# A two-layer hybrid block on one core: the modulation's products pinned in VectorE's order, spread at new paces, and cut where a condition is unused

## The chip, the cores and the metric

The kernel runs on one core of one Trainium2 chip. The metric is the device time of one execution in microseconds, the median of several executions. The engines are called by the profile's names: PE (TensorE), PEld (its weight loads), DVE (VectorE), ACT (ScalarE), POOL (GpSimd) and SP (SyncE, which issues the DMAs). A line is called by its number in the kernel before: L495 is line 495.

## The reference, cut to what matters

Two layers work on 512 latent tokens (`x`) and 256 context tokens (`xc`) of 1024 features. Each layer first makes six modulation vectors for each of two conditions, `c` for the latent tokens and `c_ctx` for the context tokens, then runs four mixers side by side and a convolutional ffn:

```python
for i in range(DEPTH):                      # DEPTH = 2
    need_ctx = i < DEPTH - 1
    mod_l = split(silu(c) @ mod_w[i] + mod_b[i], 6)
    mod_c = split(silu(c_ctx) @ mod_w[i] + mod_b[i], 6)
    h_l = modulate(x, norm_mix_g[i], mod_l[0], mod_l[1])       # shift, scale
    h_c = modulate(xc, norm_mix_g[i], mod_c[0], mod_c[1])
    ...                                     # the mixers on h_l @ w_in[i], h_c @ w_in[i]
    x = x + mod_l[2] * (o_l @ w_out[i])                        # gate
    if need_ctx:
        xc = xc + mod_c[2] * (o_c @ w_out[i])
    x = x + mod_l[5] * conv_ffn(modulate(x, norm_ffn_g[i], mod_l[3], mod_l[4]), ...)
    if need_ctx:
        xc = xc + mod_c[5] * conv_ffn(modulate(xc, norm_ffn_g[i], mod_c[3], mod_c[4]), ...)
return x
```

In the last layer (`need_ctx` false) the context tokens are still normed and projected, as keys, values and states for the latent ones, but they have no output, gate or ffn.

## The kernel before, in words

**Layout.** Activations lie as [feature, token], 128 features on the partitions: 8 blocks of 1024 features, 768 tokens. On-chip memory is 30 slabs of 1536 columns that an allocator (`Arena`) hands out and takes back while the program is traced. Each product of matrices is made of three matmuls over a rounded part and a rest of each factor (`mm_feat`, L387). A weight comes in over SP's queue into one of three staging buffers (`weights`, L371), ACT rounds it (L377), POOL subtracts for the rest (L378), and both parts go into a ring of four slabs.

**Streams and clocks.** The order of the program is made by `weave`: generators run by turns, and the one whose clock is behind goes next. A generator advances its own clock by what it yields, a cost in nanoseconds written out by hand. Within the first layer's `weave` of the mixers there are five streams: the delta rule, gated linear attention (gla), the attentions, the projections, and `mod_part(0, 16, 48, 3500)`. The projections' clock goes on by 7776 for each of 11 feature blocks and by 6 x 2640 for each of 7 token blocks (L703). In the next `weave` the stream `last` does the output product, the norm, the ffn and the next layer's norm, and beside it `next_mod` waits for the flag "normed" and runs `mod_part(1, 0, 48, 8000)`. Within the ffn's clock each of 22 up steps yields twice 7800 and each of 8 parts of a down step over four blocks 4000; the last down step goes over six blocks. What is traced is then put into each engine's queue by a scheduler that works with its own forecast of times: an instruction that it holds to be ready may be queued ahead of others that were traced earlier. Each engine takes its queue in order, SP too.

**The modulation.** The 48 blocks of 128 modulation features of a layer are, eight at a time: shift, scale and gate of the mixers, then shift, scale and gate of the ffn. The first 16 blocks of the first layer are made at the very start (`mod_first`). All others are made on DVE by `mod_part`: a block's weights come as two loads of 128 x 512 on SP's queue (L493) into four buffers taken by turns, and for each of them and each of two conditions one SCALAR_TENSOR_TENSOR (L495) multiplies by the condition's silu and sums along the row into an accumulator. These are called products below. In the profile each product has two records, the operation and the read of its accumulator. When all blocks are done, two wide operations (L500, L501) add the halves and the bias. `silu_c` loads the two condition rows, makes their silu and keeps them in `self.sc` (two tiles of 1024 columns); `mod_part` frees them at its end, and `next_mod` makes them again.

**The ffn** (L593 to L678). An up step makes a block `u`, copies it (L610), makes a block `g`, convolves it over neighbouring tokens (ACT L617; DVE L620, L622), takes its silu (ACT L626; DVE L627, L628), and splits the result (ACT L631, POOL L632). After five up steps a down step multiplies the first four by their part of `w_down` and adds the product times the gate to `x` (DVE L651). The gate is half of the modulation vector 5, made by two operations (L603) at the ffn's start.

**The norm** takes its scale from the modulation by one operation (`scales`, L534); PE sums its squares (L547).

Of the kernel before, what the change touches and what calls it, by code (L numbers as in the profile page):

```python
# [16 lines left out]
ALU = mybir.AluOpType  # L17
# [3 lines left out]
L = 2  # L21
# [12 lines left out]
# per-partition parameter columns of one layer  # L34
# [8 lines left out]
# rows that are spread over the partitions  # L43
# [8 lines left out]
# blocks of w_in's columns: ("f", columns) gives [feature, token], ("t", columns) gives [token, feature]  # L52
# [21 lines left out]
# the first 16 blocks of the first layer's mod_w, and the engine of each  # L74
# [3 lines left out]
def _ptile(a):  # L78
    """[..., K*128] -> [..., 128, K]"""
    a = np.asarray(a)  # L80
    return np.moveaxis(a.reshape(a.shape[:-1] + (-1, P)), -1, -2)


def _kmajor(w):
    """[L, K*128, N] -> [L, 128, K, N]"""
    w = np.asarray(w)
    return w.reshape(w.shape[0], -1, P, w.shape[2]).transpose(0, 2, 1, 3)
# [75 lines left out]
class Arena:  # L163
    """column ranges of equal slabs, the longest unused first; a slab without tenants may change its kind"""
# [13 lines left out]
    def find(self, n, kind, low):  # L178
        """(slab, start) of n granules whose last use is the oldest, with a price on broken slabs"""
# [39 lines left out]
class Net:  # L219
# [3 lines left out]
    # per layer: the streams' paces (delta rule, its directions, gated linear attention, attentions, projections, modulation);  # L223
    # slabs that have to be unused before a step (front, direction, attention's part, its queries)
# [23 lines left out]
    # memory --------------------------------------------------------------  # L248
# [22 lines left out]
    def bank(self, n, lo, hi):  # L271
        """waits for n banks in a row out of lo .. hi - 1"""
# [27 lines left out]
    def weave(self, *streams, pace=(1.0,) * 8):  # L300
        """emits generators by turns: the one whose clock is behind goes first"""
# [12 lines left out]
    # constants and parameters -------------------------------------------  # L314
# [25 lines left out]
    # weights -------------------------------------------------------------  # L340
    def rings(self, slabs, stages):
        """buffers that weights take by turns"""
# [9 lines left out]
    def piece(self, n):  # L352
        """the next n columns of the ring, out of one slab"""
# [8 lines left out]
    def weights(self, src, nk, n):  # L362
        """nk blocks [128, n] of a weight: lists of their rounded and rest parts"""
# [17 lines left out]
    def mm_feat(self, ps, w, x, segs, cols=slice(None)):  # L381
        """ps[:, segments] = sum over k of w[k][:, cols]^T x[k], each product of two parts of two"""
# [7 lines left out]
    def mm_part(self, ps, w, x, spans, segs):  # L390
        """mm_feat, by spans that may become ready one after the other"""
        for a, b, _ in spans:
            self.mm_feat(ps, w, x, [(a, b)])
        if not spans:
            self.mm_feat(ps, w, x, segs)

    # rsqrt of a small tile by the bit estimate and Newton steps ----------
# [11 lines left out]
    def rstd(self, ms, mean, nm, eps=EPS):  # L409
        """(ms * mean + eps) ** -0.5 of a small tile"""  # L410
# [18 lines left out]
    # modulation ----------------------------------------------------------  # L429
# [6 lines left out]
    def silu_c(self):  # L436
        """silu of both conditions' rows, on all partitions"""
# [8 lines left out]
    def mod_first(self):  # L446
        """the first layer's shift and scale of the mixers, eight features' blocks by turns, over three engines"""
# [35 lines left out]
    def mod_part(self, li, m0, m1, dt):  # L483
        """blocks m0 .. m1 - 1 of 128 columns each: shift, scale, gate of the mixers, then of the ffn, eight blocks each"""
# [4 lines left out]
        part = self.new([m1 - m0, 2, 2])  # L489
        for m in range(m0, m1):  # L490
            for e in range(2):
                w = ws[(2 * m + e) % len(ws)]
                nc.sync.dma_start(out=w, in_=self.A["modw"][li * 48 + m - 16][:, e * hd:(e + 1) * hd])  # L493
                for s in range(2):
                    nc.vector.scalar_tensor_tensor(out=junk, in0=w, scalar=1.0, in1=self.sc[s][:, e * hd:(e + 1) * hd],  # L495
                                                   op0=ALU.mult, op1=ALU.mult, accum_out=part[:, m - m0, e, s:s + 1])
                yield dt / 2
        self.free(*ws, junk, *self.sc)
        mb = self.par(li, "modb", m0, m1 - m0)
        nc.vector.tensor_tensor(out=md[:, m0:m1], in0=part[:, :, 0], in1=mb.unsqueeze(2).to_broadcast([P, m1 - m0, 2]), op=ALU.add)  # L500
        nc.vector.tensor_tensor(out=md[:, m0:m1], in0=part[:, :, 1], in1=md[:, m0:m1], op=ALU.add)  # L501
        self.free(part)
        yield 100
# [5 lines left out]
    # norm and modulation: h = rms(x) * g * (1 + scale) + shift, split -----  # L509
    @staticmethod  # L510
    def spans(full):
        """ranges of tokens with their condition, two that may run one after the other"""
        return [(0, NL, 0), (NL, T, 1)] if full else [(0, NL // 2, 0), (NL // 2, NL, 0)]

    def squares(self, x, k, a, b, st):
        """adds the squares of x[k][:, a:b] to st["acc"], but for the last one's"""
# [10 lines left out]
    def norm(self, li, which, x, sts, h, parts, first=None):  # L527
        """the parts' spans one part after the other, each with its squares"""
        nc = self.nc
        sh, sc = (0, 1) if which == "nmg" else (3, 4)  # L530
        gs = self.small([P, 8, 2], "gs")

        def scales(k, m):
            nc.vector.scalar_tensor_tensor(out=gs[:, k:k + m], in0=self.mod[li][:, sc * 8 + k:sc * 8 + k + m], scalar=1.0,  # L534
                                           in1=self.par(li, which, k, m).unsqueeze(2).to_broadcast([P, m, 2]),
# [56 lines left out]
    # conv ffn --------------------------------------------------------------  # L592
    def ffn(self, li, x, h, done):  # L593
# [8 lines left out]
        for s in range(2):  # L602
# [1256 lines left out]
```

## Time and profile before

| | us |
|---|---|
| runs of the kernel before, median of 3 | 2450.39 |
| lowest and highest of them | 2445.48 and 2453.73 |
| span of the profiled execution, first to last instruction | 2445.8 |
| PE busy in it | 2211.0 (90%) |
| DVE busy | 1490.5 (61%) |
| POOL busy | 1047.3 (43%) |
| ACT busy | 937.5 (38%) |

Of the profiled execution only the span is given, no time of its own beside it. The span is 4.6 us below the median of the runs and inside their spread. Busy shares are means over stages that differ; the rows further down give them by stage. `PEclk` or "granted clock" is the share of TensorE's full clock that the chip granted; the clock has two levels, 1.2 and 2.4 GHz, so a mean between 0.5 and 1 is a mixture.

### The profile page before, as it was taken

What the parts mean: (1) busy time and instruction counts of PE and PEld (TensorE: products, weight loads), DVE (VectorE), ACT (ScalarE), POOL (GpSimd) and SP (SyncE); (2) the same over time, 40 slices, a digit from 0 to 9 for tenths busy, and PEclk for the clock granted to TensorE, in tenths of its full rate; (3) what the DMA queues carried; (4) which work ended last, traced back from release to release, by engine and by line L of the source; (5) the groups of instructions that cost most, each with busy time, mean ns of one, the idle gap of its engine ahead of it and who ended that gap; (6) DMA issues with size and microseconds to landing.
All of it is one profiled execution on the core that took longest, in us unless ns stands there. A gap on an engine that the chain in (4) does not pass through costs nothing. (4 is left out here: it accounts for less than half of the span.)

```text
span 2445.8 us, 40328 instructions
## 1 busy us (share of the span) xinstructions
PE 2211.0 (90%) x15292; PEld 1881.8 (77%) x15292; DVE 1490.5 (61%) x3201; ACT 937.5 (38%) x1758; POOL 1047.3 (43%) x1001
## 2 busy tenths in 40 slices
PE   4879898789979998969999999997989889999999
PEld 4767687677857787858888888786878778888888
DVE  6997568678764499994222262367778874423223
ACT  3322222256546342212232344323256564533333
POOL 3442356334221253334343464346433413555556
PEclk9889888799979999989999999898889999999999
DMA  7443134433224334542211142125533232222324
GB/s 250 168 151 119 47 126 121 109 95 84 74 73 139 101 113 148 172 153 70 67 63 61 61 157 70 48 67 148 135 90 83 59 122 95 87 94 95 98 93 138
DMA packets 232434, 259.54 MB, mean 106 GB/s; under 512 B 90992, under 2 KB 174256, under 8 KB 232240
## 3 DMA queue, kind: packets, MB, share of 16 engines
q1 hardware_dynamic: 232240, 256.97, 33.8%
q8 instruction: 120, 1.97, 0.3%
q14 instruction: 74, 0.61, 0.1%
HBM read 210.74 MB, written 37.77 MB: 102 GB/s over the span
## 5 line engine op out<-in xcount | busy, mean ns | idle before, releaser
L387 PE MATMUL pst<-slab,slab 128*128 128x512 f32 (+1 forms) x6552 | 1255.3, 353 | 55.0 <-ACT slab L631 20.8
L387 PEld LDWEIGHTS pst<-slab,slab 128*128 128x128 f32 x6552 | 1065.0, 193 | 239.3 <-ACT slab L631 21.4
L378 POOL TENSOR_TENSOR slab<-slab,slab 128x512 fp32r<-128x512 f32 (+1 forms) x428 | 584.0, 1374 | 728.5 <-ACT slab L377 685.0
L377 ACT CAST slab<-slab 128x512 fp32r<-128x512 f32 (+1 forms) x428 | 257.8, 612 | 538.0 <-PE pst L387 397.5
L703 PE MATMUL pst<-slab,slab 128*128 128x256 f32 (+1 forms) x1872 | 261.8, 302 | 17.9 <-POOL slab L378 17.7
L703 PEld LDWEIGHTS pst<-slab,slab 128*128 128x128 f32 x1872 | 250.4, 205 | 27.8 <-POOL slab L378 19.5
L620 DVE SCALAR_TENSOR_TENSOR slab<-pst,pp,slab 128x511 f32<-128x511 f32 x66 | 41.5, 657 | 312.6 <-ACT slab L617 312.6
L495 DVE SCALAR_TENSOR_TENSOR slab<-slab,slab 128x512 bf16<-128x512 f32 x240 | 227.6, 948 | 6.9 <-DMA slab<-in_modw_dram 0.8
L427 PE MATMUL pst<-cst,slab 128*128 128x128 f32 (+1 forms) x968 | 166.5, 305 | 60.0 <-POOL slab L1148 16.6
L427 PEld LDWEIGHTS pst<-cst,slab 128*128 128x128 f32 (+1 forms) x968 | 121.0, 153 | 88.0 <-DVE slab L859 20.0
L1545 PE MATMUL pst<-slab,slab 128*128 128x128 f32 (+5 forms) x1376 | 162.1, 278 | 9.1 <-DVE slab L1599 4.8
L651 DVE SCALAR_TENSOR_TENSOR slab<-pst,fgate,slab 128x512 f32<-128x512 f32 (+1 forms) x144 | 88.0, 629 | 127.5 <-PE pst L387 127.4
L1545 PEld LDWEIGHTS pst<-slab,slab 128*128 128x128 f32 (+3 forms) x1376 | 135.1, 176 | 29.8 <-issue 14.4
L940 DVE TENSOR_REDUCE mx<-pst 128x1 f32<-128x768 f32 (+1 forms) x120 | 100.2, 846 | 43.3 <-PE pst L937 20.6
L942 ACT ACTIVATE slab<-pst,mx 128x768 f32<-128x768 f32 (+1 forms) x120 | 97.9, 817 | 50.9 <-DVE mx L940 50.1
L632 POOL TENSOR_TENSOR slab<-slab,slab 128x768 fp32r<-128x768 f32 (+1 forms) x44 | 71.2, 1618 | 97.9 <-ACT slab L631 94.4
L626 ACT ACTIVATE slab<-slab 128x768 f32<-128x768 f32 (+1 forms) x44 | 32.4, 737 | 144.2 <-DVE slab L622 144.2
L495 DVE SCALAR_TENSOR_TENSOR slab<-slab 128x512 bf16<-128x512 f32 x80 | 73.5, 918 | 2.3
L1577 POOL TENSOR_TENSOR slab<-slab,pc 128x256 f32<-128x256 f32 x48 | 34.3, 727 | 87.6 <-PE pst L1545 16.0
L953 ACT ACTIVATE slab<-slab,r 128x768 f32<-128x768 f32 (+1 forms) x80 | 67.7, 853 | 8.7 <-DVE r L952 8.1
L970 PE MATMUL pst<-slab,slab 128*64 128x128 f32 x816 | 64.7, 291 | 3.8 <-ACT slab L422 1.7
L631 ACT CAST slab<-slab 128x768 fp32r<-128x768 f32 (+1 forms) x44 | 32.0, 728 | 92.1 <-DVE slab L628 92.0
(309 smaller groups left out, 2689.7 us busy)
## 6 DMA issues: line engine op xcount, KB each, us to landing
slab<-in_wup_dram SPq DMA_DIRECT2D x88, 512.0 KB, 3.4
slab<-in_modw_dram SPq DMA_DIRECT2D x160, 256.0 KB, 2.6
slab<-in_wdn_dram SPq DMA_DIRECT2D x48, 512.0 KB, 3.4
slab<-in_win_dram SPq DMA_DIRECT2D x46, 512.0 KB, 3.6
slab<-in_modw_dram SPq DMA_DIRECT2D x16, 512.0 KB, 7.0
slab<-in_wout_dram SPq DMA_DIRECT2D x16, 512.0 KB, 3.5
slab<-in_xT_dram SPq DMA_DIRECT2D x16, 384.0 KB, 5.7
kb<-slab SPq DMA_DIRECT2D x8, 768.0 KB, 4.2
```

The lines of the kernel that those rows point to most:

```text
L377: nc.scalar.copy(out=w[0], in_=st[:, k:k + q])
L378: nc.gpsimd.tensor_tensor(out=w[1], in0=st[:, k:k + q], in1=w[0].bitcast(F32), op=ALU.subtract)
L387: self.nc.tensor.matmul(ps[:, a:b], w[i][k][:, cols], x[j][k][:, a:b], start=(k == 0 and q == 0), stop=(k == nk - 1 and q == 2))
L427: self.nc.tensor.transpose(out, a.bitcast(F32) if a.dtype != F32 else a, self.c["ident"])
L495: nc.vector.scalar_tensor_tensor(out=junk, in0=w, scalar=1.0, in1=self.sc[s][:, e * hd:(e + 1) * hd], op0=ALU.mult, op1=ALU.mult, accum_ou ...
L632: nc.gpsimd.tensor_tensor(out=HL[:, 1, :n], in0=th[:, :n], in1=HL[:, 0, :n].bitcast(F32), op=ALU.subtract)
L651: nc.vector.scalar_tensor_tensor(out=x[m][:, a:b], in0=ps[:, a:b], scalar=gate[:, m, s:s + 1], in1=x[m][:, a:b], op0=ALU.mult, op1=ALU.add)
L703: self.nc.tensor.matmul(ps[:, :n], h[i][k][:, t * P:(t + 1) * P], w[j][k], start=(k == 0 and q == 0), stop=(k == KD - 1 and q == 2))
L940: nc.vector.tensor_reduce(out=mx, in_=sv, axis=AX.XY, op=ALU.max, negate=True)
L942: nc.scalar.activation(out=p[m][:, a:].rearrange("p (e c) -> p e c", e=2 - a // hb), in_=sv, func=AF.Exp, bias=mx, accum_out=lsum[:, m:m + 1])
L953: nc.scalar.activation(out=p[0][:, a:], in_=p[0][:, a:], func=AF.Copy, scale=r[:, 0:1])
L1545: mm = lambda o, a, b, pos: nc.tensor.matmul(o, a, b, start=True, stop=True, tile_position=pos)
```

## The change

`mod_part` takes a list of blocks instead of a range, adds the halves and the bias block by block, and no longer frees the condition rows. Each product is passed through the framework's `keep_in_program_order`, which adds an edge from the instruction that was traced last on the same engine: the product may not be queued on DVE ahead of it. The edge orders the queue and adds no semaphore wait. `conds` says how many conditions a block is made for: two, but one for the gates and the ffn's vectors of the last layer.

The blocks move. Beside the first layer's mixers run only blocks 16 to 39, at 8000 per block instead of 3500. Blocks 40 to 47, the first layer's ffn gate, run beside its ffn at 6000 per block, and behind them the 48 blocks of layer 2 at 9500 instead of 8000. The gate's two operations move from the ffn's start to the end of its fourth up step, behind a wait in the tracing for the flag "ffn gate". The silu of the conditions is made once.

```diff
-    def mod_part(self, li, m0, m1, dt):
+    def mod_part(self, li, ms, dt):
...
-        part = self.new([m1 - m0, 2, 2])
-        for m in range(m0, m1):
+        part = self.new([len(ms), 2, 2])
+        for i, m in enumerate(ms):
+            n = self.conds(li, m // 8)
             for e in range(2):
-                w = ws[(2 * m + e) % len(ws)]
+                w = ws[(2 * i + e) % len(ws)]
                 nc.sync.dma_start(out=w, in_=self.A["modw"][li * 48 + m - 16][:, e * hd:(e + 1) * hd])
-                for s in range(2):
-                    nc.vector.scalar_tensor_tensor(out=junk, in0=w, scalar=1.0, in1=self.sc[s][:, e * hd:(e + 1) * hd],
-                                                   op0=ALU.mult, op1=ALU.mult, accum_out=part[:, m - m0, e, s:s + 1])
+                for s in range(n):
+                    self.tc.keep_in_program_order(nc.vector.scalar_tensor_tensor(
+                        out=junk, in0=w, scalar=1.0, in1=self.sc[s][:, e * hd:(e + 1) * hd],
+                        op0=ALU.mult, op1=ALU.mult, accum_out=part[:, i, e, s:s + 1]))
                 yield dt / 2
-        self.free(*ws, junk, *self.sc)
-        mb = self.par(li, "modb", m0, m1 - m0)
-        nc.vector.tensor_tensor(out=md[:, m0:m1], in0=part[:, :, 0], in1=mb.unsqueeze(2).to_broadcast([P, m1 - m0, 2]), op=ALU.add)
-        nc.vector.tensor_tensor(out=md[:, m0:m1], in0=part[:, :, 1], in1=md[:, m0:m1], op=ALU.add)
-        self.free(part)
-        yield 100
+            nc.vector.scalar_tensor_tensor(out=md[:, m, :n], in0=part[:, i, 0, :n], scalar=self.par(li, "modb", m),
+                                           in1=part[:, i, 1, :n], op0=ALU.add, op1=ALU.add)
+        self.free(*ws, junk, part)
+
+    @staticmethod
+    def conds(li, part):
+        return 2 if li < L - 1 or part < 2 else 1
...
     def ffn(self, li, x, h, done, S):
         gate = self.small([P, 8, 2], "fgate")
-        for s in range(2):
-            nc.vector.tensor_scalar(out=gate[:, :, s], in0=self.modvec(li, 5, s), scalar1=0.5, scalar2=None, op0=ALU.mult)
...
             acts.append((yield from up(i)))
             todo.append(i)
+            if i == 3:
+                yield from self.wait(S, "ffn gate")
+                for s in range(self.conds(li, 5)):
+                    nc.vector.tensor_scalar(out=gate[:, :, s], in0=self.modvec(li, 5, s), scalar1=0.5, scalar2=None, op0=ALU.mult)
...
-    def next_mod(self, li, S):
+    def ffn_mod(self, S):
         yield from self.wait(S, "normed")
-        self.silu_c()
-        yield from self.mod_part(li, 0, 48, 8000)
+        yield from self.mod_part(0, range(40, 48), 6000)
+        S["ffn gate"] = True
+        yield from self.mod_part(1, range(48), 9500)
+        self.free(*self.sc)
...
-                streams.append(self.mod_part(0, 16, 48, 3500))
+                streams.append(self.mod_part(0, range(16, 40), 8000))
...
-                streams.append(self.next_mod(li + 1, S))
+                streams.append(self.ffn_mod(S))
+            else:
+                S["ffn gate"] = True
```

`scales` in the norm takes the number of conditions from `conds` too. The rest of the diff takes out comments.

## Rows read from the trace of the kernel before

**Rows 1.** The page: busy tenths in 40 slices of the span, and the granted clock.

```profile
PE   4879898789979998969999999997989889999999
...
DVE  6997568678764499994222262367778874423223
...
PEclk9889888799979999989999999898889999999999
```

**Rows 2.** Windows in the first ffn: stretch, length, busy us (records) by engine, clock, DMA share, GB/s.

```profile
857.00:1105.00 248.00, 215.35 (x1163) 184.53 (x1164) 241.79 (x480) 64.86 (x101) 100.39 (x60) 0.93 0.43 145
1105.00:1425.00 320.00, 320.00 (x1817) 278.75 (x1816) 98.36 (x138) 91.13 (x134) 136.15 (x98) 1.00 0.22 70
```

**Rows 3.** Windows of L495 alone: stretch, length, DVE busy us (records), clock, DMA share, GB/s.

```profile
85.00:280.00 195.00, 119.94 (x256) 0.89 0.41 137
...
857.00:1105.00 248.00, 181.89 (x382) 0.93 0.43 145
```

**Rows 4.** PE's waits from 855 to 1105 us, the longest: us in total, times, longest.

```profile
PE pst L387 <- ACT slab L631: 20.8, 2, 13.9
```

**Rows 5.** Timeline, 1058 to 1082 us: start, us, engine, line, count, idle before and releaser.

```profile
1059.60 11.09 SPq L493 DMA_DIRECT2D slab<-in_modw_dram  x6
1059.61 2.22 DVE L495 SCALAR_TENSOR_TENSOR slab<-slab,slab 128x512 bf16<-128x512 f32 x1
...
1065.23 0.69 DVE L495 SCALAR_TENSOR_TENSOR slab<-slab,slab 128x512 bf16<-128x512 f32 x1
...
1070.74 0.43 SPq L371 DMA_DIRECT2D slab<-in_wdn_dram  x1
...
1071.72 1.13 DVE L620 SCALAR_TENSOR_TENSOR slab<-pst,pp,slab 128x511 f32<-128x511 f32 x2
...
1074.00 0.84 ACT L626 ACTIVATE slab<-slab 128x768 f32<-128x768 f32 x1 [12.27 <-DVE slab L622]
...
1075.43 1.81 POOL L378 TENSOR_TENSOR slab<-slab,slab 128x512 fp32r<-128x512 f32 x1 [10.79 <-ACT slab L377]
...
1079.63 1.01 PE L387 MATMUL pst<-slab,slab 128*128 128x512 f32 x2 [13.90 <-ACT slab L631]
```

**Rows 6.** Windows of the mixers' starts, layers 1 and 2: columns as in rows 2.

```profile
85.00:280.00 195.00, 158.95 (x1215) 134.08 (x1214) 168.90 (x373) 56.57 (x93) 85.17 (x58) 0.89 0.41 137
280.00:450.00 170.00, 156.08 (x1206) 137.26 (x1205) 102.23 (x221) 40.63 (x90) 85.35 (x89) 0.85 0.37 106
...
1467.00:1640.00 173.00, 165.09 (x1289) 139.70 (x1288) 66.03 (x145) 63.58 (x108) 74.99 (x66) 0.96 0.17 57
```

**Rows 7.** PE's waits for DVE, from 85 to 250 and from 280 to 460 us.

```profile
PE pst L1122 <- DVE slab L1114: 9.9, 1, 9.9
...
PE pst L1545 <- DVE slab L1599: 1.9, 1, 1.9
```

**Rows 8.** Windows of L703 alone, around 450 us: PE and PEld busy us.

```profile
425.00:450.00 25.00, 16.90 (x113) 15.88 (x111) 0.82 0.51 115
450.00:475.00 25.00, 0.00 (x0) 0.00 (x0) 0.73 0.35 100
```

**Rows 9.** Line L534: ns min/median/max, first and last start.

```profile
L534 DVE SCALAR_TENSOR_TENSOR gs<-mod,pp x11: 144/160/2292, 32.7 to 1108.8; 128x2 f32<-128x2 f32 x8, 128x16 f32<-128x16 f32 x3
```

**Rows 10.** Groups of POOL, L378: 857 to 1105 us, then 1105 to 1425 us.

```profile
L378 POOL TENSOR_TENSOR slab<-slab,slab 128x512 fp32r<-128x512 f32 x46 | 76.5, 1680 | 94.7 <-ACT slab L377 84.5 <-issue 10.1
...
L378 POOL TENSOR_TENSOR slab<-slab,slab 128x512 fp32r<-128x512 f32 x85 | 114.4, 1350 | 166.1 <-ACT slab L377 166.0
```

**Rows 11.** SP queue's waits for products: the whole span, then 80 to 450 us.

```profile
SPq L493 <- DVE slab L495: 251.3, 138, 8.2
...
SPq L493 <- DVE slab L495: 90.3, 48, 8.2
```

**Rows 12.** PE's timeline: the norm between the layers.

```profile
1451.65 2.74 PE L547 MATMUL pst<-cst,slab 128*128 128x1 f32 x24
```

More of the change, by code (lines that the diff above doesn't have):

```diff
@@ L531, in norm @@
         gs = self.small([P, 8, 2], "gs")
+        nco = self.conds(li, sc)
         def scales(k, m):
-            nc.vector.scalar_tensor_tensor(out=gs[:, k:k + m], in0=self.mod[li][:, sc * 8 + k:sc * 8 + k + m], scalar=1.0,
-                                           in1=self.par(li, which, k, m).unsqueeze(2).to_broadcast([P, m, 2]),
+            nc.vector.scalar_tensor_tensor(out=gs[:, k:k + m, :nco], in0=self.mod[li][:, sc * 8 + k:sc * 8 + k + m, :nco], scalar=1.0,
+                                           in1=self.par(li, which, k, m).unsqueeze(2).to_broadcast([P, m, nco]),
                                            op0=ALU.add, op1=ALU.mult)
@@ L590, in norm, with ffn @@
             self.free(rs)
-    def ffn(self, li, x, h, done):
+    def ffn(self, li, x, h, done, S):
         nc = self.nc
@@ L1813, in done @@
                     nc.sync.dma_start(out=self.out[:, m, a:b], in_=x[m][:, a:b])
-            yield from self.ffn(li, x, hf, done)
+            yield from self.ffn(li, x, hf, done, S)
             if li < L - 1:
```

## The prediction

> **What bounds the kernel now.** I read the page's 40 slices first, then the windows, then the waits and the timeline of the worst place. In the slices [rows 1] TensorE (PE) is near full almost everywhere, and VectorE (DVE) is at nine tenths in slices 1 and 2 (61 to 183 us) and 14 to 17 (856 to 1100 us; slices counted from 0). The reader is to see that in slices 2 and 17 DVE stands at 9 while PE falls to 7 and 6 and its clock to 8 tenths. So a full DVE takes time from PE in two places, and the question is how much.
>
> The windows answer it [rows 2]. From 857 to 1105 us of the ffn PE issues 1163 matmuls in 248 us at a granted clock of 0.93; from 1105 to 1425, the rest of the same ffn, 1817 in 320 us without a pause at 1.00, that is 5.68 per us. At that rate 1163 need 205 us. **The first part loses 43 us**: 248.00 - 215.35 = 33 idle and 10 from matmuls at the clock's lower level, 1.2 GHz. What is different there is L495, the modulation products: 181.89 us of DVE in that part [rows 3], or 0.95 us for each product (382 records, half of them the accumulator's read).
>
> The waits name a release by ACT L631 for 20.8 us of the idle time [rows 4], the rounding of an ffn activation. The timeline shows what is late behind it [rows 5]. On SP's queue a group of six loads for L495 takes 11.09 us, since each waits for a buffer that DVE has not read; the weight load L371 behind it goes out at 1070.74, ACT and GpSimd (POOL) wait for it, POOL 10.79 us. On DVE the convolution L620 runs only at 1071.72, behind a row of products; ACT L626 waited 12.27 us for it, and PE stands 13.90 us. One cause, a DVE that the scheduler has filled with products that no one needs yet, has two ways to PE.
>
> The other place is the start of layer 1's mixers. From 85 to 280 us PE is busy 158.95 of 195; layer 2's same stretch (the end of the gla blocks' start, the delta rule's projections), which has no products, takes 173 us for more matmuls, 1289 against 1215 [rows 6]. PE waits there 9.9 us for a DVE copy [rows 7] that stands behind products.
>
> **The change, part by part.**
>
> 1. *Fewer products.* Before: 32 blocks x 4 + 48 x 4 = 320. After: 24 x 4 + 8 x 4 + 16 x 4 + 32 x 2 = 256, with 24 x 2 + 56 x 2 = 160 loads as before. 64 x 0.95 = 61 us less on DVE, none of it on the path by itself. The second computation of silu (two loads, four DVE operations) goes too: its DVE time is part of the saturated stretch counted below.
>
> 2. *ffn of layer 1: order and pace.* The products now stand where they are traced, behind what DVE was given before them. The ffn stream's own clock is 96 matmuls per 15.6 us; at 5.68 per us that is 16.9 us, a factor of 1.083. DVE without products is 98.36 of 320 us, 0.31 [rows 2]. Gate blocks: 4 x 0.95 every 6.5 us adds 0.58, in all 0.89 for 8 blocks (52 us). Layer 2's shift and scale: 3.8 every 10.3 us, 0.68. The other 32: 0.50. Nowhere above 1, so neither way to PE is left; products lag at most by the convolution they stand behind. The activations have a whole further up step in hand before a down step reads them, and DVE needs about 0.31 x 16.9 = 5 us of each step. Of the 43 us I keep 2 for the first down step, which comes soon after the dense part: **-41**, bounds -43 and 0. Next late is nothing but PE itself, as from 1105 on.
>
> 3. *Wait for the gate.* The ffn stream waits at its fourth up step's end, at 62.4 us of its clock; eight blocks end at 48. It adds nothing, and the gate's two small operations move off the ffn's start. If the products lag, the first down step's L651 waits, not its matmuls.
>
> 4. *Mixers of layer 1.* 24 blocks at 8 us each are 192 us of stream clock. The projections' clock is 11 x 7.8 + 7 x 15.8 = 196 us, and their last matmuls (L703) end just before 450 us [rows 8]. So products should lie from 86 to about 445 us, 96 x 0.95 = 91 us, a density of 0.25 where it was 119.94/195 = 0.62 [rows 3]. At layer 2's rate 1215 matmuls take 163 us, so up to 32 us can come back; the density falls by 0.59, which gives -19. Against that 0.46 of the products, 42 us, now lie between 280 and 450, where DVE is 0.60 busy and goes to 0.85. Bounds: nothing (PE waits there 1.9 us for DVE [rows 7]), or what a microsecond of products cost before, 32/120 x 42 = 11; I take the middle, +6. **-13**, bounds -32 and +11. The two condition rows stay in memory until the ffn's end, 2048 columns of 30 slabs of 1536, so a step that asks for unused slabs may be traced later, beside other streams that go on; no row prices that, and I take nothing.
>
> 5. *Small sums.* 80 products' sums of 128x1 or x2 replace four wide operations. The row nearest to them is L534, 0.16 us in the median, 2.29 at most [rows 9]: 13 us of DVE at the median, hidden as above.
>
> 6. *Layer 1 to 2.* The stream of products ends at 48 + 48 x 9.5 = 504 us, the ffn at 22 x 15.6 + 4 x 32 + 21 = 492 and the next norm's tracing at 504. So about 7 products stand in the last step and the norm, 2 of them in the norm where DVE sets the pace: **+2**, bounds 0 and 7.
>
> Sum: -41 - 13 + 2 = -52. The profiled execution's span of 2445.8 becomes 2394; it lies 4.6 us under the median of the three runs, 2450.4, and the forecast is for the median: **2398 us**.
>
> **Rivals.**
>
> *Everything comes back (0.15).* Layer 1's start becomes as clean as layer 2's: -43 - 32 = -75, 2375 us. For it: the stretches are alike. Against: a quarter of DVE still goes to products.
>
> *The mixers gain nothing (0.17).* Products only move to where rope and the delta rule's features want DVE: -41 + 11 + 2 = -28, 2422 us.
>
> *The pin does not hold (0.05).* If the scheduler still brings all products forward, 160 x 0.95 = 152 us of them end near 1064, before the 13.90 us stall: about half of the 43 remains, 2428 us.
>
> *DVE and POOL block each other (0.09).* In one stretch a product takes 2.22 and another 0.69 us [rows 5], and POOL's L378 takes 1.68 us beside products and 1.35 without [rows 10]. If every product met a subtraction it would take 0.69 + 1.35 + 0.08 = 2.1 us: a gate block needs 8.4 + 2.0 us of DVE per 6.5, behind by 31 us after eight, and sixteen more at 11.6 per 10.3 add 21. A lag over one up step of 16.9 us reaches PE, so some 35 of the 41 us stay: 2433 us. The mean of 0.95 speaks against it: few products meet one. The Trainium skill ("SBUF — State Buffer", section "SBUF: two separate sides") speaks for it: the port pair that VectorE and GpSimd share is an exclusive lock, and the loser blocks for a whole instruction. The two durations agree with that; how often they meet, only the mean says.
>
> *The queue becomes the wait (0.10), slower.* A product pinned behind a DVE operation that waits for PE keeps its buffer; the load for it then holds SP's queue, and with it the weights and the mixers' loads behind. L493 waited 138 times, 1.8 us each, for products already before, 48 of them (90.3 us) in the first stretch [rows 11]. If all 48 loads of the mixers now held what is behind them for 1.8 us, that is 86 us: 2450 - 41 + 86 = 2495. It decides from 23 of the 48 on. Against it: products at half the rate, two blocks of buffers ahead.
>
> **How the numbers follow.** The forecast has 0.44. The range, 2368 to 2436, takes in all cases but the last and leaves 0.2 with the forecast's own tails: the mixers' order is laid out anew. 0.3% is 7.4 us, about what a measurement can tell from no change. The cases on the faster side hold 0.90; of these I move 0.07 to the others, since a new order of the mixers can take back more than its bound. Faster by more 0.83, within it 0.06, slower 0.11.
>
> **What would show it.** Right: 256 products, the last of the mixers' near 445 us and of the ffn's near 1380; DVE at 0.9 or less; 2980 matmuls of the ffn at 5.6 per us or better; PE's first step of the next norm (L547), now at 1451.65 [rows 12], near 1400. Wrong: L387 still waiting for L631 in the ffn (the pin or the port), L371 standing behind L493 (the queue), or the norm before the first ffn later than now (the mixers).

## The result, and the profile after

| | before | after |
|---|---|---|
| median of 4 runs each, us | 2448.11 | 2409.04 |
| ratio, with its 95% interval | | 0.9832 [0.9805, 0.986] |
| span of the profiled execution, us | 2445.8 | 2408.0 |
| first PE step of the norm before the first ffn, us | 845.2 | 833.3 |
| first PE step of the norm between the layers | 1451.65 | 1403.69 |
| first PE step of the norm before the last ffn | 2071.1 | 2033.3 |

The kernel is 39 us faster; 2398 was forecast. (The ratio is a statistic of its own; the quotient of the two medians is 0.984.) The three norms cut the span into four stretches, which the rest of the text uses. By the profiled executions the mixers of layer 1 (from the start to the first norm) became 11.9 us shorter, the first ffn with its norm 36.1 shorter (606.5 to 570.4), the mixers of layer 2 10.2 **longer** (619.4 to 629.6), and the last ffn stayed (374.7 to 374.6). Each of these is one execution. Where two kernels have nearly the same order of instructions in a stretch, the traces show how far one stretch varies by itself: the mixers of layer 1 end at 833.3, 835.4 and 837.9 (after, e4, e11) and at 835.1 and 830.4 (e2, e7), and the mixers of layer 2 take 615.6 to 622.8 (before, e2, e7, e8) and 632.6 and 627.4 (e9, e12). So some 7 us of a difference in a stretch of the mixers can be chance. The first ffn varies less: with the products pinned and no pause put in, it lies between 569.7 and 572.0. The comment lines that the change takes out move the numbers: L497 is the product (L495 before) and L495 its load, L501 a block's sum, L552 the norm's squares (L547), L566 the norm's next step (L561), L634 the activation's rounding (L631), L710 and L1552 the token blocks and the delta rule's matmuls (L703, L1545), L866 rope's copy (L859).

The page after, to be held against [rows 1]:

```profile
PE   4889988789988999999999989998899889999999
...
DVE  6855689877774388655544662469777865322323
...
PEclk9889988688989999999999999998899899999999
```

DVE's two full places are gone, but slice 6 (361 to 421 us), where [rows 1] has 8, is now at 9: DVE is busy there for 54.75 of 60 us, only 12.71 of them with products. Slice 7 (421 to 482 us) stands out too: the clock falls to 6 tenths, while PE stays at 7; [rows 1] has 7 for both there. PE's timeline in the first ffn after, which answers to the 13.90 us in [rows 5] (start, us, engine, line, count, idle before and releaser):

```profile
842.20 561.65 PE L387 MATMUL pst<-slab,slab 128*128 128x512 f32 x3168 [0.74 <-ACT slab L583]
```

One row holds the whole ffn: no gap long enough to end it. PE's waits in it come to 0.7 us, in the kernel before to 34.2. The windows after, whole kernel, columns as in [rows 2], for the two parts of that ffn, one stretch inside it, and the mixers of layer 1 up to the last projection and from there to the norm:

```profile
842.00:950.00 108.00, 107.69 (x595) 92.56 (x596) 92.22 (x176) 42.17 (x66) 51.39 (x35) 0.98 0.39 120
950.00:1404.00 454.00, 454.00 (x2579) 394.67 (x2577) 252.60 (x450) 131.71 (x200) 199.04 (x136) 1.00 0.40 125
1057.00:1342.00 285.00, 285.00 (x1615) 247.17 (x1615) 140.24 (x248) 78.93 (x115) 115.33 (x78) 1.00 0.37 114
...
24.00:418.00 394.00, 347.62 (x2565) 300.22 (x2566) 288.51 (x631) 116.94 (x222) 193.93 (x152) 0.91 0.39 124
418.00:833.00 415.00, 364.67 (x3012) 301.77 (x3012) 277.83 (x705) 207.93 (x444) 121.68 (x195) 0.89 0.33 91
```

The same for the kernel before, whose projections end at 449 us:

```profile
1105.00:1390.00 285.00, 285.00 (x1647) 249.23 (x1646) 84.86 (x123) 79.12 (x116) 114.03 (x82) 1.00 0.21 67
...
24.00:449.00 425.00, 361.37 (x2584) 311.04 (x2585) 322.58 (x683) 117.46 (x223) 200.30 (x160) 0.88 0.40 130
449.00:845.00 396.00, 346.39 (x2992) 286.11 (x2991) 272.32 (x698) 205.72 (x442) 117.73 (x188) 0.92 0.32 91
```

Three things are to be seen. In the ffn DVE is no longer a limit (92.22 of 108, then 252.60 of 454). Over the same length and at the same clock of 1.00, with no pause in either, PE issues **1615 matmuls after and 1647 before**; that is taken up at the end. And in the mixers the first stretch is 31 us shorter and the second 19 us longer.

### The profile page after: what moved, and what is told of

The parts are those of the page before. It is cut to its first block, busy times and chain, and to the rows that moved or that the text cites. A ratio compares the mean times of both kernels' runs of the same rounds, so it can differ in the third digit from the quotient of the medians.

```text
span 2408.0 us, 40175 instructions
## 1 busy us (share of the span) xinstructions
PE 2209.1 (92%) x15292; PEld 1880.6 (78%) x15292; DVE 1457.9 (61%) x3144; ACT 938.8 (39%) x1756; POOL 1040.0 (43%) x1001
## 4 chain that ended last, share of the span: by engine, by line
PE 63%; DVE 6%; POOL 4%; ACT 3%; issue 3%; DMA 2%; SPq 0%; POOLq 0%; DVEq 0%; ACTq 0%
PE pst L387 44%; PE pst L1552 5%; PE pst L427 4%; PE pst L710 3%; PE pst L977 2%; PE pst L1670 1%; PE pst L1675 1%; PE pst L941 1%; DVE mx L947 1%; ACT slab L949 1%; PE pst L944 1%; POOL slab L378 1%; DMA of<-slab 1%; POOL slab L846 0%; PE pst L1207 0%
## 5 line engine op out<-in xcount | busy, mean ns | idle before, releaser
L387 PEld LDWEIGHTS pst<-slab,slab 128*128 128x128 f32 x6552 | 1056.2, 191 | 201.5 <-ACT slab L583 10.8
L378 POOL TENSOR_TENSOR slab<-slab,slab 128x512 fp32r<-128x512 f32 (+1 forms) x428 | 576.8, 1357 | 724.1 <-ACT slab L377 701.9
L710 PE MATMUL pst<-slab,slab 128*128 128x256 f32 (+1 forms) x1872 | 260.4, 300 | 11.0 <-POOL slab L378 11.0
L710 PEld LDWEIGHTS pst<-slab,slab 128*128 128x128 f32 x1872 | 249.1, 204 | 20.1 <-POOL slab L378 12.4
L497 DVE SCALAR_TENSOR_TENSOR slab<-slab,slab 128x512 bf16<-128x512 f32 x208 | 194.6, 936 | 6.1 <-DMA slab<-in_modw_dram 2.9
L1552 PE MATMUL pst<-slab,slab 128*128 128x128 f32 (+4 forms) x1328 | 167.3, 291 | 12.8 <-DVE slab L1606 4.0
L1552 PEld LDWEIGHTS pst<-slab,slab 128*128 128x128 f32 (+3 forms) x1328 | 139.6, 186 | 35.3 <-issue 10.5
L634 ACT CAST slab<-slab 128x768 fp32r<-128x768 f32 (+1 forms) x44 | 32.2, 732 | 84.1 <-DVE slab L631 84.0
L1639 POOL TENSOR_TENSOR slab<-cst,pcu 64x256 f32<-64x256 f32 x48 | 32.3, 673 | 72.7 <-PE pst L1552 18.5
L1425 DVE TENSOR_TENSOR slab<-slab,slab 96x31 f32<-96x31 f32 (+15 forms) x124 | 57.0, 459 | 8.7 <-DMA slab<-scrin 7.1
```

Of the source, the lines that this page charges most:

```text
L378: nc.gpsimd.tensor_tensor(out=w[1], in0=st[:, k:k + q], in1=w[0].bitcast(F32), op=ALU.subtract)
L387: self.nc.tensor.matmul(ps[:, a:b], w[i][k][:, cols], x[j][k][:, a:b], start=(k == 0 and q == 0), stop=(k == nk - 1 and q == 2))
L497: self.tc.keep_in_program_order(nc.vector.scalar_tensor_tensor(out=junk, in0=w, scalar=1.0, in1=self.sc[s][:, e * hd:(e + 1) * hd], op0=AL ...
L710: self.nc.tensor.matmul(ps[:, :n], h[i][k][:, t * P:(t + 1) * P], w[j][k], start=(k == 0 and q == 0), stop=(k == KD - 1 and q == 2))
L1552: mm = lambda o, a, b, pos: nc.tensor.matmul(o, a, b, start=True, stop=True, tile_position=pos)
```

## Experiments

The theory at the start: the pin alone frees the ffn, the spread of the blocks frees the mixers' start and takes part of it back later, and the paces at the ffn's end cost the transition. The rivals: the paces do the ffn's part, the dropped condition does some of it, or the mixers' stretches have little to do with the products.

**e1, the change without its pin.**

```diff
-                    self.tc.keep_in_program_order(nc.vector.scalar_tensor_tensor(
-                        out=junk, in0=w, scalar=1.0, in1=self.sc[s][:, e * hd:(e + 1) * hd],
-                        op0=ALU.mult, op1=ALU.mult, accum_out=part[:, i, e, s:s + 1]))
+                    nc.vector.scalar_tensor_tensor(
+                        out=junk, in0=w, scalar=1.0, in1=self.sc[s][:, e * hd:(e + 1) * hd],
+                        op0=ALU.mult, op1=ALU.mult, accum_out=part[:, i, e, s:s + 1])
```

> The changed kernel without the pin: the products may be queued on DVE ahead of what was traced before them; counts, paces and places stay. If the order is what counts (my step 2): the 160 products of the ffn come forward, DVE is over nine tenths for about 150 us from 845 us on, PE stands between 10 and 20 us in the first ffn, and the time is 2420 to 2435 us. If fewer products at a slower pace do it alone: PE stands under 3 us in the ffn and the time stays at 2409 within 4.

Measured: 2446.01 us, above the 2420 to 2435 expected, ratio 0.9999 [0.998, 1.0018]; the ffn took 600.6 us, and PE stood for 29.9 of them instead of 10 to 20. The two longest waits in PE's timeline:

```profile
949.21 1.01 PE L387 MATMUL pst<-slab,slab 128*128 128x512 f32 x2 [8.21 <-ACT slab L634]
...
1076.09 1.01 PE L387 MATMUL pst<-slab,slab 128*128 128x512 f32 x2 [10.75 <-ACT slab L634]
```

The waits of [rows 4] are back, for the same rounding. The larger of the two groups of the ffn's products shows why (ns min/median/max, first and last start):

```profile
L497 DVE SCALAR_TENSOR_TENSOR slab<-slab,slab x136: 675/691/2334, 863.8 to 1072.5; 128x512 bf16<-128x512 f32 x136
```

Products are over by 1074 us, whatever pace they were traced at. Without the pin the new paces and the 64 missing products are worth nothing that the ratio can show.

**e2, the pin alone on the kernel before.**

```diff
-                    nc.vector.scalar_tensor_tensor(out=junk, in0=w, scalar=1.0, in1=self.sc[s][:, e * hd:(e + 1) * hd],
-                                                   op0=ALU.mult, op1=ALU.mult, accum_out=part[:, m - m0, e, s:s + 1])
+                    self.tc.keep_in_program_order(nc.vector.scalar_tensor_tensor(out=junk, in0=w, scalar=1.0, in1=self.sc[s][:, e * hd:(e + 1) * hd],
+                                                   op0=ALU.mult, op1=ALU.mult, accum_out=part[:, m - m0, e, s:s + 1]))
```

> The kernel before with the pin and nothing else: 320 products, the old paces, the wide sums, the gate at the ffn's start. If the order counts: at 8000 per block the ffn's density is 4 x 0.95 / 8.67 = 0.44 beside 0.31 of other work, so PE does not stand in the ffn and the 36 us come back; the mixers at 3500 gain 0 to 6; no product stands in the step between the layers. 2402 to 2412 us. If fewer products and other paces are needed: PE still stands over 15 us in the ffn and the time is over 2430 us.

Measured: 2394.27 us, below the 2402 to 2412 expected, ratio 0.9794 [0.9772, 0.9817]. The ffn takes 570.7 us, as after, and PE's timeline shows no pause in it:

```profile
861.02 544.91 PE L387 MATMUL pst<-slab,slab 128*128 128x256 f32 x3097 [0.50 <-POOL slab L585]
```

The mixers of layer 1 are 10.1 us shorter than before, where 0 to 6 was expected, those of layer 2 (619.5) as before. **One line does all of the gain.** By the medians it beats the whole change by 15 us, and each of its four runs is faster than each of the four after; by the ratios (0.9794 and 0.9832, whose intervals overlap a little) it is 9 us.

**e8, the pin on the ffn's products only.**

```diff
-                    nc.vector.scalar_tensor_tensor(...
+                    (self.tc.keep_in_program_order if li else (lambda i: i))(nc.vector.scalar_tensor_tensor(...
```

> The kernel before with the pin on the products beside the first ffn only; those beside the mixers float as before. It splits e2's gain. If the two places add up: the first norm of the ffn at 845 as before, the ffn's segment (norm to norm) 570 as in e2, the next 620: about 2410 us. If the pin beside the mixers is what gains: ffn 600 or more, the time near 2440.

Measured, in a single run: 2407.27 us, ffn 570.6, first norm at 844.8. The two places add up: the ffn's 36 us, and about 10 from the pin beside the mixers at the old pace.

**e7, the pin and the dropped condition.** Layer 2's blocks from 16 on are made for one condition, as in the change (the sums, the norm's scales and the pin, as in e2, are not shown).

```diff
-                for s in range(2):
+                for s in range(2 if li == 0 or m < 16 else 1):
```

> The kernel with the pin alone (e2) and the unused condition dropped: 64 products fewer, all in the first ffn. If dropping products is worth nothing by itself once their order is pinned (my step 1): within 4 us of e2's 2394. If their count still matters in the ffn: 5 us or more below it.

Measured: 2396.47 us, 0.9793 [0.9777, 0.981], beside 0.9794 for e2. Sixty-four products less on an engine with room are worth nothing that can be told apart here.

**e4, layer 2's blocks at 9000**, so that they end before the ffn does.

```diff
-        yield from self.mod_part(1, range(48), 9500)
+        yield from self.mod_part(1, range(48), 9000)
```

> Layer 2's blocks in the first ffn at 9000 per block instead of 9500: the stream of products ends at 48 + 432 = 480 us of its clock, before the ffn's 492. If the products in the step between the layers cost what I read there (PE's wait of 4.6 us for a sum of squares behind two products): the step from the first L552 to L566 takes 5.2 us as before the change instead of 10.8, and the time is 2402 to 2405 us. If the products lag behind their clock, or the time goes elsewhere: 2409 within 3.

Measured: 2404.53 us, 0.9837 [0.9809, 0.9864]. In the timelines of the norm between the layers, first after:

```profile
1406.17 1.74 DVE L497 SCALAR_TENSOR_TENSOR slab<-slab,slab 128x512 bf16<-128x512 f32 x1
...
1410.15 1.87 PE L552 MATMUL pst<-cst,slab 128*128 128x1 f32 x8 [4.62 <-DVE slab L526]
```

then e4:

```profile
1406.30 2.74 PE L552 MATMUL pst<-cst,slab 128*128 128x1 f32 x24
1411.53 2.93 PE L566 MATMUL pst<-slab,cst 128*128 128x512 f32 x4 [2.50 <-DVE slab L563]
```

The median cannot be told from the 2409.04 of after, but the lines can. After, two products stand between the squares' sums on DVE and PE waits 4.62 us; from L552 to L566 it takes 10.8 us, in e4 5.2, as in the kernel before. The mixers of layer 2 came to 620.9.

**e3, no blocks beside layer 1's mixers.** The 24 blocks are set to zero, so this kernel leaves out the mixers' gate and the ffn's shift and scale of layer 1.

```diff
-                streams.append(self.mod_part(0, range(16, 40), 8000))
+                nc.vector.memset(self.mod[0][:, 16:40], 0.0)
```

> The changed kernel without the 24 blocks beside the first layer's mixers (their 48 features' blocks 16 to 39 are set to zero, so the first layer's mixer gate and its ffn's shift and scale are left out). It shows what is left of my bound of 32 us for the mixers, of which the change took 12. If the products beside the mixers still cost by their share: the first norm of the ffn, now at 833.3 us, comes 10 to 20 us earlier. If a quarter of DVE is free there: within 4 us of 833.

Measured, in a single run: 2395.18 us. The first norm came 34 us earlier than after (799.1), beyond both expectations, but the mixers of layer 2, whose code is the same, took 647.2 us instead of 629.6. So the 24 blocks cost 34 us where they stand; DVE's instructions in layer 2's mixers stand in another order than after, and 18 us are lost there.

**e5 and e6, the 24 blocks denser and thinner**, both on e4.

```diff
-                streams.append(self.mod_part(0, range(16, 40), 8000))
+                streams.append(self.mod_part(0, range(16, 40), 3500))
```

> The kernel of e4 with the 24 blocks beside the mixers at the old 3500 per block instead of 8000. After the change and in e4 the stretch from the projections' last matmul to the first norm of the ffn takes 415 us, before the change 396, with the pin alone 398, without any products there 395. If it is the products that stand between 280 and 420 us that delay the delta rule and the attentions' start (my +6, too small): the projections end 5 to 15 us later than e4's 420, the stretch falls to 395 to 402, the norm comes at 818 to 830, the time is 2388 to 2400 us. If it is the condition rows that stay in memory: the stretch stays at 410 to 418 and the time does not fall below e4's 2404.

```diff
+                streams.append(self.mod_part(0, range(16, 40), 15500))
```

> The kernel of e4 with those 24 blocks at 15500, so that they are spread over all of the mixers' stage (372 of 397 us of stream clock), a density of about 0.12. If what products cost grows with their share of DVE, as my step 4 has it: the first norm of the ffn comes before e4's 835, at 815 to 830, and the time is under 2400 us. If a product beside the delta rule and the attentions costs about its own length wherever it stands: the norm at 835 to 855 us, the time 2404 to 2425 us.

Measured: 2405.56 us, 0.9832 [0.9807, 0.9856], and 2406.39, 0.9834 [0.9813, 0.9855]; e4 had 0.9837. The first norm came at 825.5 and 826.5 (e4: 835.4), and the mixers of layer 2, laid out anew, lost most or all of it again (635.4 and 627.5 beside 620.9). So the norm moved as the first expectation of each said, and the time, not under 2400, did not. Denser and thinner bring the norm forward alike, so it does not follow the density.

**e9, the condition rows freed after the mixers and made again, as before**, on e4.

```diff
-                streams.append(self.mod_part(0, range(16, 40), 8000))
+                streams.append(self.mixers_mod(8000))
...
+    def mixers_mod(self, dt):
+        yield from self.mod_part(0, range(16, 40), dt)
+        self.free(*self.sc)
...
         yield from self.wait(S, "normed")
+        self.silu_c()
```

> The kernel e4_pace9000 (2404.5 us, ffn blocks of layer 2 at 9000) with the two condition rows freed when the mixers' 24 blocks are done and made again at the ffn's start, as the kernel before has it; the products, their places and paces stay. Theory A: the rows held in memory delay steps that ask for unused slabs, and that is what lengthened the stretch from the projections' end to the norm from 396 to 415 us: it comes back to 396 to 402 and the norm before the first ffn stands at 815 to 822; the time is 2388 to 2396. Theory B: the products that stand beside the delta rule and the attentions do it: the stretch stays at 410 to 418 and the time at 2401 to 2408. The rows made again cost four DVE operations in a stretch that has room: at most 3 us by either.

Measured: **2387.16 us, 0.9741 [0.9713, 0.977], the fastest version of the study.** The norm came at 813.8, 394.0 us after the last projection: a little better than theory A's numbers, and e10 tries them once more.

**e10, the same at 3500.**

```diff
-                streams.append(self.mixers_mod(8000))
+                streams.append(self.mixers_mod(3500))
```

> The kernel e9_freed_rows with the mixers' 24 blocks at 3500 for a block as in e5_mix3500, so that both the rows are free and the products are over by about 280 us. By theory A and B together the stretch from the projections' end to the norm is that of the kernel before, 396 to 402 us; with the projections' end of e5 (423) the norm stands at 819 to 825 and the time at 2388 to 2398. If neither sets the stretch, but the order that the scheduler happens to lay out, it lies anywhere from 395 to 418, and the layer-2 mixers, whose code no edit touches, again move by 10 us or more.

Measured: 2421.58 us, 0.9887 [0.9853, 0.992]; norm at 840.8, 419.4 us after the last projection. Theory A falls as a general cause: the rows are free here too, and the stretch is the longest of all. Rows and pace together give 415 (e4), 403 (e5), 394 (e9) and 419 (e10): neither acts the same way in both pairs.

What the good and the bad orders differ in, the windows from the last projection to the norm show, first e9, then e10:

```profile
420.00:813.00 393.00, 343.85 (x3003) 282.52 (x3003) 275.73 (x709) 205.60 (x444) 121.85 (x190) 0.93 0.35 96
```

```profile
421.00:840.00 419.00, 365.52 (x3048) 301.25 (x3047) 273.00 (x702) 209.45 (x449) 116.58 (x181) 0.89 0.32 90
```

PE's idle time is 49.2 us in e9 and 53.5 in e10; before it was 396 - 346.39 = 49.6 and after 50.3. It hardly differs. What differs is PE's **busy** time for nearly the same matmuls: 343.9 (e9), 346.4 (before), 364.7 (after) and 365.5 us (e10), at a granted clock of 0.93, 0.92, 0.89 and 0.89. With two levels, 2 x (1 - 0.92) x 396 = 63 us of the stretch lay at the lower one before and 2 x (1 - 0.89) x 415 = 91 us after; if work there takes twice as long, an estimate, these 28 us cost up to 14 of the 18 that PE was busy longer. The groups of the delta rule's matmuls in that stretch, before and then after (count, busy us, mean ns, idle before):

```profile
L1545 PE MATMUL pst<-slab,slab 128*128 128x128 f32 (+3 forms) x680 | 78.1, 273 | 3.4 <-DVE slab L1599 1.9 <-ACT slab L1607 1.4
```

```profile
L1552 PE MATMUL pst<-slab,slab 128*128 128x128 f32 (+3 forms) x712 | 93.9, 304 | 10.9 <-DVE slab L1606 4.0 <-DVE slab L1578 3.6 <-ACT slab L1598 1.4
```

The same kind of work takes 304 ns a matmul instead of 273: 15.8 us more busy time here alone, of which the 32 more matmuls account for about 4 (at 78.1/680 us each). It is worst right behind the last projection, in windows of the kernel before and then of after:

```profile
449.00:530.00 81.00, 57.20 (x458) 45.34 (x457) 69.67 (x172) 38.71 (x80) 27.36 (x53) 0.83 0.39 100
```

```profile
418.00:500.00 82.00, 59.98 (x358) 47.70 (x357) 61.27 (x159) 30.80 (x63) 27.46 (x52) 0.65 0.44 110
```

With the projections over, PE has only short chains with gaps between them; after, those 82 us ran at a clock of 0.65 and PE got through 358 matmuls instead of 458. By the same sum the lower level held for 28 of the 81 us and for 57 of the 82, so about all of the difference lies here. Why the gaps fell so in one order and not in another is not shown.

**e11, a pause put into the ffn**, on e4, for the 1615 and 1647 matmuls above: 44 needless copies of the fourth activation onto itself, ahead of the first down step.

```diff
             todo.append(i)
+            if full and i == 3:
+                for _ in range(44):
+                    nc.scalar.copy(out=acts[3][:, 0, :n], in_=acts[3][:, 0, :n].bitcast(F32))
```

> The kernel e4_pace9000 (2404.5 us) with 44 needless copies of the fourth activation in place on ScalarE (44 x 0.84 = 37 us) ahead of the first down step of the first ffn, so that TensorE runs out of work there for some 10 to 25 us. Theory: TensorE's cadence at a full granted clock changes at a long pause, as it did in the kernel before (16.97 us for an up step of 96 matmuls until the pause of 13.9 us, 16.64 after it): after the pause here an up step takes 16.64 us, and the 480 us behind it give back about 9 us of the pause. Rival: the cadence has nothing to do with pauses and stays at 16.97 us to the ffn's end; the ffn is then longer by the whole pause.

Measured, in a single run: 2428.66 us. PE stood for 27.2 us, and the ffn was 22.3 us longer than in e4 (593.2 to 570.9):

```profile
975.13 456.11 PE L387 MATMUL pst<-slab,slab 128*128 128x512 f32 x2616 [27.20 <-ACT slab L679]
```

The windows of e4 and then of e11, behind the pause:

```profile
980.00:1040.00 60.00, 60.00 (x341) 52.08 (x340) 39.27 (x67) 18.23 (x26) 25.77 (x17) 1.00 0.34 109
```

```profile
980.00:1040.00 60.00, 60.00 (x347) 52.90 (x347) 39.52 (x80) 14.95 (x23) 21.69 (x16) 1.00 0.39 123
```

From one matmul's start to the next, per 256 columns, it is 117.8 ns in e4's ffn from 875 us to its last down step and in e11's from there to the pause, and 115.6 from the pause to there. The order of PE's matmuls in the ffn is the same in both. In this run the theory holds; the lower clock around the pause (0.77 from 920 to 980) took part of what came back.

**e12, a short pause**: the copies of e11, 17 instead of 44, on e9.

```diff
-                for _ in range(44):
+                for _ in range(17):
```

> The kernel e9_freed_rows (2387.2 us) with 17 of the needless copies of e11_stall instead of 44, so 27 x 0.83 = 22.4 us less of the pause of 27.2: about 5 us. Theory A, any pause resets TensorE's cadence: an up step takes 16.64 us behind it instead of 16.97, the 450 us behind the pause give back 8 to 9 us and cost 5 and a little of the lower clock; the ffn (569.7 in e9) takes 565 to 570. Theory B, it takes a pause long enough for the granted clock to fall (13.9 and 27.2 us did): the cadence stays at 16.97 and the ffn takes 574 to 576, the time 2391 to 2393.

Measured: 2398.42 us, 0.9786 [0.9762, 0.9809]; ffn 583.2 (e9: 569.7). PE stood for 3.68 and 4.92 us, the granted clock was 0.89 and 0.88 in the two stretches of 30 us around them, and the cadence stayed at 117.8 ns. So not any pause changes it, and theory B's condition is not it either, since the clock fell here too. The cost, 13.5 us, was also more than its 4 to 6 (574 to 576 less 569.7): the pauses are 8.6, and the rest is put down to matmuls at the lower clock.

## Why the prediction was right, and where it was not

The sum was -52 and the profiled span changed by -37.8. Sign and place hold, and so does the mechanism in the ffn; in the mixers the sum came out by luck. Three terms were mis-sized.

1. *Fewer products, nothing on the path.* Right: e7 beside e2 shows it.

2. *ffn, -41.* Measured **-36.1**. The pin holds, PE does not pause, and DVE keeps room. The new paces were not needed for it: e2 has the old one. That "next late is nothing but PE itself" was right; that PE would then go "as from 1105 on" was not. After the pause at 1065 us the kernel before ran 1.9% quicker, at 115.6 ns per 256 columns; after stays at 117.8. Over the 285 us shown that is 32 matmuls, or 32/1615 x 285 = 5.6 us, enough for the 4.9 that are missing. The step took its rate of 5.68 per us from that quicker part. The pause that the change removed had been paying back part of itself, and in e11 a pause did so again.

3. *The gate's wait, 0.* Right: those 0.7 us are all that PE waits in the ffn after, and they are for ACT L583, which is not the gate.

4. *Mixers, -13.* Measured -11.9, right as a sum and **wrong in both its parts**; that two errors of 12 and 13 us cancel is luck. The term "-19" for the stretch before the last projection measured -31 (425 to 394), near the bound of -32: 17 of idle time and 14 of PE's busy time. The "+6" for later work measured +19, beyond its bound of 11. That step priced products standing before DVE's other work. But the idle time of the last stretch did not grow (49.6 and 50.3); its matmuls ran at the lower clock more often, which no term had. Nor did the products lie as forecast: the last one ended at 417, just as the projections did, not near 445, and DVE, forecast at 0.85, was busy for 120.73 of the 138 us from 280 to 418, 0.87, and for 0.91 of slice 6, just past the sign of 0.9 or less. Nor was the lower density needed for it: in e2, at the old pace, the projections end at 437 and the stretch behind them takes 398, together 10.1 less than before. Beside e2, the rest of the change moved the projections' end 18 us forward, and the stretch behind it grew by 17. Keeping the condition rows, taken as nothing, may or may not matter: freed, the stretch is shorter at one pace (e9) and longer at the other (e10). What makes an order of the mixers good is open.

5. *Small sums.* L501 took 221 ns in the median instead of 160; hidden as forecast, in a DVE with room.

6. *Transition, +2.* Measured **+10.2** for the stretch, of which 5.6 is the wait that was named (bounds 0 to 7) and e4 takes away. The last product ran at 1426.5, not near 1380. The other 4.6 lies in the mixers of layer 2, where no edit touches an instruction. It cannot be told from chance: e1, whose order behind the norm is that of after, took 622.1, and the order of before alone spans 7 us. Between kernels of other orders that stretch lay anywhere from 615.6 to 647.2 us.

The rivals. *The pin does not hold* fell, and e1 shows that its price was near: 2428 was worked out for products that end near 1064, and without the pin they ended at 1074, at 2446. *The queue becomes the wait* fell: no PE wait in the ffn has to do with L371. SP waited for products 164.5 us over the span instead of 251.3 [rows 11], and another 99.7 for a block's sum, so no less in all:

```profile
SPq L495 <- DVE slab L497: 164.5, 80, 10.7
SPq L495 <- DVE mod L501: 99.7, 41, 13.1
```

*DVE and POOL block each other* fell as a price: in the ffn a product took (47.96 + 96.60)/157 = 0.92 us on average, by the windows of L497 alone (842 to 950 and 950 to 1404 us), and PE never waited for it. The longest product of that ffn took 2.21 us and the median 0.69, which agrees with the exclusive lock that the Trainium skill ("SBUF — State Buffer", section "SBUF: two separate sides") describes; no row counts such meetings, but none made PE wait in that ffn. *The mixers gain nothing* and *everything comes back* are out by the -11.9, whatever its parts.

## What to carry to other kernels

If the scheduler may take filler work forward, its pace in the trace may decide nothing, as in e1: order it behind the work that it stands beside first, and only then tune paces. Count what a stretch gives back in PE's busy time as well as in its idle time: here some 3000 matmuls between gaps cost 344 us at a clock of 0.93 and 365 at 0.89. And run the smallest part of a change by itself: here one line beat the whole, and a reordering of the rest gave anything from a ratio of 0.9741 (e9) to 0.9887 (e10), with 0.9837 for e4, without a rule that these runs could find. A single execution says little there: with one and the same order a stretch moved by 5 to 7 us.

## What the hardware showed unexpectedly

At a granted clock of 1.00 and without any wait, the same matmuls of the ffn, in the same order, run at one of two cadences, 117.8 or 115.6 ns per 256 columns. By the matmuls' starts most of it lies in those of 512 columns: from such a start to the next it is 236.4 ns in the 285 us of after and 231.6 in those of before, from a start of 256 columns 116.9 and 115.0. The quicker one set in behind pauses of 13.9 us (before), 10.75 (e1) and 27.2 (e11), the slower one stayed behind 4.92 (e12) and in the ffns of after, e2, e4 and e9, which never paused. Behind e1's 8.21 us it was 115.6 for the 6 us at the full clock before the next short pauses, and the slower one was back after those. What switches it is not shown. Neither pause that was put in paid for itself: e11's 27.2 us came back to 22.3, and e12's 8.6 grew to 13.5.
